# Pairs of experts in one result bank: zero columns in the stationary operand, split weights in the common buffers, a smaller gather, and a shift that VectorE adds

## The chip, the core and the metric

One core of one Trainium2 chip runs the whole program. The metric is the device time of one execution in microseconds (us). The engines are TensorE (PE, with its weight loads as PEld), VectorE (DVE), ScalarE (ACT), GpSimd (POOL) and SyncE (SP), which issues the transfers (DMA) of the weights.

## What is computed

Two transformer blocks on 256 tokens of 1024 features. The first mixes three branches and has a dense feed-forward layer; the second has two kinds of attention and a mixture of 32 experts, and the change lies in that last part. Each token goes to the best of 4 groups and there to its best 2 of 8 experts:

```python
h2 = _modulate(_rmsnorm(x, g_ffn), shift_ffn, scale_ffn)       # x * gain + shift, per feature
group = argmax(h2 @ w_group);  top_p, top_local = top_k(softmax(expert logits of the group), 2)
y[dest] = (silu(xb @ w_gate[e]) * (xb @ w_up[e])) @ w_down[e]   # 1024 -> 512 -> 1024, every expert e
x = x + gate_ffn * (weighted sum of each token's two expert rows)
```

All is float32. The weights of the experts are 32 x 6 pieces of 1 MiB.

## The kernel before

**Weights as a stream of units.** `PLAN` lists 319 units, each 128 x 2048 float32 (1 MiB), in the order of their use; the last 192 are those of the experts. I number these 0 to 191. They come as: 8 units of gate and up weights of a pair of experts (2 + 2 for each of the two), then 4 units of down weights of the pair before, and so on; so a pair has 12 units. `prefetch` (L295) issues one transfer per unit on SP while fewer than `st["cap"]` raw units are held and the pool `units` (18 buffers, `NS`) has one free. The cap is 13 before the experts and 7 in them (L1249, L1549).

**Two parts of a weight.** PE multiplies rounded operands (fp32r) in one pass. So that nothing is lost, `convert_unit` (L330) splits a unit: ACT writes `hi`, the rounded weight, and DVE writes `lo = raw - hi` (L345). Then each unit is used by 4 matmuls with `hi` and 4 with `lo`, 128 x 512 of weights moving in each. `hi` has 3 buffers, `lo` 2, in a pool of their own, `pairs`. The function `whole` (L290) names the units that are not split: PE multiplies them as plain float32, by 8 matmul instructions that take longer. It picks units 13, 37, 61, ..., eight in all.

**An expert's rows.** An expert has 32 slots for tokens. `gather` (L1408) multiplies the normed tokens (`hth`, `htl`, rounded part and remainder) by a matrix of zeros and ones (`oh`, made by DVE) and so brings the rows of 8 experts at once into `xg`: 32 columns of rounded parts and 32 of remainders per expert, 64 columns in all. These 64 columns stand still in PE while the weights move, so a result has 64 partitions. `gate_up` (L1476) writes the gate and up results of one expert into one bank each (`pe`), and ACT copies each to `gy` (64 x 512). `hidden` (L1489) folds the two halves of a pair together on PE (`pT`), and ACT and DVE make `hs`, the input of the down weights. `down` (L1510) writes two banks per expert (`pd`), and ACT copies them to `gy`.

**Other work between the units.** Generators in the list `bg` are pulled one step at each half unit: `gather` of the next 8 experts (every 4 pairs), `put_weights` (the routing weights, every 4 pairs), and `put_back` (L1526), which after every 4 pairs returns 4 pairs' results to the tokens by 64 float32 matmul instructions (`py`); DVE adds these to `x` (L1539). Copies and sums that wait for PE are put off by `post` for a number of half units.

**Order.** The order on each engine is made by a scheduler when the program is built, within the dependences and the buffers; SP keeps the order in which the code issues. Each engine works strictly in that order.

**Before the experts.** The routing stretch computes the logits, picks groups and experts on DVE, and makes the normed tokens: for each of four tiles, 4 matmuls of `x` with a diagonal of gains (`dg`) and one matmul that adds the shift (`std` times `shift_row`, one row), then `hth` on ACT and `htl` on DVE straight from the bank (L1359 to L1370).

Of the kernel before, what the change touches and what calls it, by code (L numbers as in the profile page):

```python
# [213 lines left out]
def block_kernel(ctx: ExitStack, tc: tile.TileContext, A, out):  # L214
# [75 lines left out]
    def whole(u):  # L290

        m = u - MOE0
        return m < NU - MOE0 - 4 and m % 24 == 13
# [36 lines left out]
    def convert_unit(parts=1):  # L330
# [20 lines left out]
    def take_unit(*name):  # L351
# [14 lines left out]
        if whole(u):  # L366
            raw.pop(u)
            free()

# [850 lines left out]
    shift_row = gains[0:1, 1024:]  # L1220
    gains = gains[:, :1024].rearrange("p (k f) -> p k f", k=8)
    for k in range(8):
        V.tensor_scalar(gains[:, k], ident, gm[:, 1, k:k + 1], None, op0=OP.mult)
    for k4 in range(2):
        p = ps("pb")
        for i in range(4):
            k = 4 * k4 + i
            mm(p[:1, i * 128:(i + 1) * 128], mod[:, 24 + k:25 + k], ident, start=True, stop=True)
        V.tensor_copy(shift_row[:, k4 * 512:(k4 + 1) * 512], p[:1])
# [19 lines left out]
    st["cap"] = 13  # L1249
# [121 lines left out]
    free()  # L1371
# [35 lines left out]

    def gather(g):  # L1408

        oh = [t256("oh", F32R) for tt in range(2)]  # L1410
        for tt in range(2):
            t1 = t256("oh1")
            V.tensor_scalar(t1, slot, slg[g][:, 0, tt:tt + 1], None, op0=OP.is_equal)
            last["oh"] = V.scalar_tensor_tensor(oh[tt], slot, slg[g][:, 1, tt:tt + 1], t1,
                                                op0=OP.is_equal, op1=OP.add).ins
        yield
        xs = [unit("xg", F32R).rearrange("p (e k c) -> p e k c", e=4, k=8) for i in range(2)]
        xg[2 * g], xg[2 * g + 1] = xs
        yield
        for k in range(8):  # L1420
            p = ps("pg")
            for i, h in enumerate((hth, htl)):
                for tt in range(2):
                    mm(p[:, i * 256:(i + 1) * 256], h[:, tt, k * 128:(k + 1) * 128], oh[tt],
                       start=i + tt == 0, stop=tt == 1, skip_group_check=True)

            def keep(k=k, p=p):
                pv = p.rearrange("p (i e r) -> p i e r", i=2, e=8)
                for i in range(2):
                    last["xg"] = act(xs[i][:, :, k].rearrange("p e (i r) -> p i e r", i=2), pv[:, :, 4 * i:4 * i + 4],  # L1430
                                     AF.Copy)
# [43 lines left out]

    def gate_up(e):  # L1476
        xs = xg[e // 4][:, e % 4]
        for i, nm in enumerate(("eg", "eu")):
            p = ps("pe")
# [3 lines left out]
            if e % 4 == 0 and not i:  # L1483
                g = unit("gy")
                gy[e // 2], gy[e // 2 + 1] = g[:, :1024], g[:, 1024:]
            t = gy[e // 2][(e % 2) * 64:(e % 2) * 64 + 64]
            post(lambda i=i, p=p, t=t: act(t[:, i * 512:(i + 1) * 512], p[:64], AF.Copy))

    def hidden(q):  # L1489
# [13 lines left out]
        def parts():  # L1503
            act(hs[:, :, :, 0], sv, AF.Copy)
            V.tensor_sub(hs[:, :, :, 1], sv, hs[:, :, :, 0])  # L1505
        post(product, 2)
        post(parts, 4)
        return hs.rearrange("p f e i r -> p f e (i r)")

    def down(e, hs):  # L1510
        pd = [ps("pd"), ps("pd")]
        for k2 in range(2):
            for ws in take_unit("ed", e, k2):
                rows_times([(pd[n][:64], hs[:, 2 * k2 + i, e % 2], 2 * i + n, k2 + i == 0, k2 + i == 2)
                            for i in range(2) for n in range(2)])(ws)
        y = gy[e // 2][(e % 2) * 64:(e % 2) * 64 + 64]

        def keep():
            for n in range(2):
                if n and e == NE - 1:  # L1520
                    V.tensor_copy(y[:, n * 512:(n + 1) * 512], pd[n][:64])
                else:
                    act(y[:, n * 512:(n + 1) * 512], pd[n][:64], AF.Copy)
        post(keep)
# [33 lines left out]
    for p in range(NE // 2 + 1):  # L1558
# [153 lines left out]
```

## Time and profile before

| | us |
|---|---|
| median of 3 runs | 1336.34 (1331.66 to 1337.39) |
| the profiled execution's own time | 1338.32 |
| its span in the trace | 1336.5 |
| PE / DVE / ACT / POOL busy in the span | 1215.3 / 1045.3 / 840.4 / 101.6 |
| bytes read | 338.88 MB |

Busy time of PE runs from a matmul's start to its modelled end, and neighbours overlap; the spacing of starts tells more. The experts' stretch, from the first matmul with an expert's weights to the last of `put_back`, lies between 755 and 1317 us. No engine is busy all of that time, so the waits have to be read beside the busy time.

### The profile page before, as it was taken

The page shows a single profiled execution, that of the slowest core. Times are in us where ns is not written, and L with a number is a line of the kernel's source. Part 1 is how long each engine was busy: PE and PEld are TensorE (multiplying, and loading weights), DVE is VectorE, ACT ScalarE, POOL GpSimd, SP SyncE. Part 2 cuts the span into 40 slices and gives each one's busy share as a digit, 9 for nine tenths or more (in the row PEclk, how much of TensorE's full clock was granted, in tenths as well). Part 3 has the DMA queues.
Part 4 walks back from the last instruction along what each step waited for, and adds up shares of the span by engine and source line. Part 5 has one row for each costly group of instructions (what it writes and reads, how often), then busy time and mean ns, then how long its engine had stood idle before and what let it go on. Part 6 is the DMA issues. An engine that isn't in the chain of part 4 may idle for free. (4 is left out here: it accounts for less than half of the span.)

```text
span 1336.5 us, 19007 instructions
## 1 busy us (share of the span) xinstructions
PE 1215.3 (91%) x7468; PEld 966.8 (72%) x7468; DVE 1045.3 (78%) x1215; ACT 840.4 (63%) x983; POOL 101.6 (8%) x102
## 2 busy tenths in 40 slices
PE   6996999999999999889999989989898988889885
PEld 6984899989999999788888645546554655456454
DVE  6799999967898887766456597986797669867874
ACT  5576545384644444554554589985887679767872
POOL 2569200200000000000000000000000000000000
PEclk8899999999999999898998799999899999999998
DMA  9632356547698885231171297998799879989921
GB/s 364 257 126 94 138 224 212 190 164 287 257 339 335 318 320 229 86 136 64 50 280 81 107 382 299 400 421 347 272 391 398 316 285 376 423 328 354 421 108 33
DMA packets 48621, 341.21 MB, mean 255 GB/s; under 512 B 5392, under 2 KB 5648, under 8 KB 7824
## 3 DMA queue, kind: packets, MB, share of 16 engines
q1 hardware_dynamic: 47664, 337.65, 65.3%
q10 hardware_dynamic: 864, 2.31, 0.5%
q8 instruction: 60, 0.98, 0.3%
q14 instruction: 33, 0.27, 0.1%
HBM read 338.88 MB, written 1.05 MB: 254 GB/s over the span
## 5 line engine op out<-in xcount | busy, mean ns | idle before, releaser
L221 ACT ACTIVATE hi<-raw 128x1024 fp32r<-128x1024 f32 (+1 forms) x392 | 562.4, 1456 | 300.2 <-issue 46.7
L345 DVE TENSOR_TENSOR lo<-raw,hi 128x2048 fp32r<-128x2048 f32 (+1 forms) x186 | 414.9, 2264 | 100.7 <-ACT hi L221 39.5
L323 DVE TENSOR_TENSOR lo<-raw,hi 128x1024 fp32r<-128x1024 f32 x206 | 260.2, 1270 | 77.6 <-ACT hi L221 77.2
L237 PE MATMUL pe<-lo,xg 128*64 128x512 f32 x480 | 133.3, 402 | 19.8 <-DVE lo L345 18.6
L237 PE MATMUL pe<-hi,xg 128*64 128x512 f32 x480 | 131.0, 401 | 7.7 <-ACT hi L221 7.7
L237 PEld LDWEIGHTS pe<-lo,xg 128*64 128x64 f32 x480 | 60.3, 135 | 76.7 <-DVE lo L345 39.2
L237 PEld LDWEIGHTS pe<-hi,xg 128*64 128x64 f32 x480 | 63.6, 136 | 57.1 <-ACT hi L221 14.2
L630 DVE SCALAR_TENSOR_TENSOR ca<-ch,par,ca 128x246 f32<-128x246 f32 (+25 forms) x180 | 101.2, 590 | 0.9
L237 PE MATMUL pd<-lo,hs 128*64 128x512 f32 x256 | 73.9, 414 | 13.5 <-DVE lo L345 12.6
L1689 POOL TENSOR_TENSOR x<-x,rstd 128x512 f32<-128x512 f32 x1 | 1.7, 1717 | 1057.3 <-DVE rstd L496 1057.3
L237 PE MATMUL pd<-hi,hs 128*64 128x512 f32 x256 | 73.3, 413 | 8.4 <-DVE hs L1505 4.5
L237 PEld LDWEIGHTS pd<-lo,hs 128*64 128x64 f32 x256 | 33.4, 139 | 47.5 <-DVE lo L345 28.5
L237 PE MATMUL py<-ws,gy 128*128 128x256 f32 x256 | 60.4, 392 | 4.5 <-PEq L1598 4.1
L237 PEld LDWEIGHTS pd<-hi,hs 128*64 128x64 f32 x256 | 34.8, 140 | 36.1 <-ACT hi L221 8.6
L237 PEld LDWEIGHTS py<-ws,gy 128*128 128x128 f32 x256 | 50.5, 198 | 14.0 <-issue 4.9
L621 POOL TENSOR_TENSOR ca<-ca,tap 128x255 f32<-128x255 f32 (+29 forms) x60 | 56.5, 944 | 35.9 <-ACT tap L221 32.3
L314 DVE SCALAR_TENSOR_TENSOR raw<-raw,aux 128x1024 f32<-128x1024 f32 x48 | 56.8, 1219 | 0.0
L221 ACT ACTIVATE gy<-pe 64x512 f32<-64x512 f32 x64 | 37.9, 592 | 27.0 <-PE pe L237 26.0
L237 PE MATMUL pgt<-nh,hi 128*128 128x256 f32 x192 | 54.3, 283 | 0.0
L237 PE MATMUL pgt<-nl,hi 128*128 128x256 f32 x192 | 54.1, 282 | 0.0
L237 PE MATMUL pgt<-nh,lo 128*128 128x256 f32 x192 | 53.8, 280 | 0.0
L221 ACT ACTIVATE gy<-pd 64x512 f32<-64x512 f32 x63 | 34.3, 583 | 29.3 <-PE pd L237 29.1
(345 smaller groups left out, 3019.2 us busy)
## 6 DMA issues: line engine op xcount, KB each, us to landing
raw<-in_ws_dram SPq DMA_DIRECT2D x318, 1024.0 KB, 7.0
x<-in_xt_dram SPq DMA_DIRECT2D x4, 256.0 KB, 4.3
raw<-in_ws_dram SPq DMA_DIRECT2D x2, 512.0 KB, 8.9
out_dram<-x SPq DMA_DIRECT2D x4, 256.0 KB, 2.7
aux<-in_sguw_dram ACTq DMA_DIRECT2D x1, 512.0 KB, 9.7
aux<-in_cnt_dram SPq DMA_DIRECT2D x1, 512.0 KB, 12.6
aux<-in_sgub_dram ACTq DMA_DIRECT2D x1, 512.0 KB, 3.9
aux<-in_cvec_dram ACTq DMA_DIRECT2D x1, 512.0 KB, 4.7
```

The costliest lines, as they stand in the source:

```text
L221: ins = S.activation(out, in_, func, **k).ins
L237: last["mm"] = T.matmul(*a, **k).ins
L314: V.scalar_tensor_tensor(r, r, 1.0, cond["c"], op0=OP.mult, op1=OP.mult, accum_out=mod[:, col:col + 1])
L323: st["lo"] = V.tensor_sub(lo, r, hi).ins
L345: st["lo"] = V.tensor_sub(lo[:, c], raw[u][:, c], hi[:, c]).ins
L621: G.tensor_tensor(ca[:, j, d:], ca[:, j, d:], t[:, :256 - d], op=OP.add)
L630: V.scalar_tensor_tensor(ca[:, j, d:], ch[:, j, :256 - d], w(30 - d), ca[:, j, d:], op0=OP.mult, op1=OP.add)
L1689: (G if k2 == 3 else V).tensor_tensor(x2, x2, over2(r), op=OP.mult)
```

## The change

Six edits go together.

1. **Pairs in one bank.** The rows of a pair stand in 192 columns (`xs`): 64 of the even expert, 64 zeros, 64 of the odd one. `window` takes 128 of them: rows and zeros for the even expert, zeros and rows for the odd one. Both experts' matmuls then accumulate into the same 128 partitions of a bank, and ACT copies a bank once per pair, 128 x 512. The input of the down weights (`hsz`) is laid out in the same way. GpSimd writes the zeros once.
2. **Split parts in the common buffers.** `hi` and `lo` are taken from `units`; each split unit holds two buffers until its matmuls are issued. The buffers of `xg` are no longer taken from there. The caps are 10 and 5 for 13 and 7.
3. **Whole units.** Units 9, 25, 41, ..., twelve in all, are not split.
4. **Gather per four experts**, every 2 pairs; the `oh` of eight experts is still made at once. A gather matmul moves 128 columns for 256, and there are 256 of them for 128.
5. **Shift.** The one-row matmul goes. The shift stands in all partitions (made by PE and ACT in the attention stretch), DVE adds it to the scaled tile (`row`), and ACT and DVE split `row` (`keep_rows`).
6. Some copies and `put_back` are put off by one or two half units more.

```diff
     def whole(u):
-        return m < NU - MOE0 - 4 and m % 24 == 13
+        return m < NU - MOE0 - 4 and m % 16 == 9
...
-            hi = pairs.tile([P, 2048], F32R, name="hi", tag="hi", bufs=3)
-            lo = pairs.tile([P, 2048], F32R, name="lo", tag="lo", bufs=2)
+            hi, lo = unit("hi", F32R), unit("lo", F32R)
...
+            t = t256("sd", shape=(P, P))
+            V.tensor_scalar(t, ident, mod[:, 24 + k:25 + k], None, op0=OP.mult)
+            mm(p[:, i * 128:(i + 1) * 128], one1, t, start=True, stop=True)
+        act(shift[:, k4 * 512:(k4 + 1) * 512], p, AF.Copy)
...
-    st["cap"] = 13
+    st["cap"] = 10
...
-                mm(p, std[:, tt * 128:(tt + 1) * 128], shift_row[:, k4 * 512:(k4 + 1) * 512], start=False, stop=True,
-                   skip_group_check=True)
-            act(hth[:, tt, c], p, AF.Copy, scale=rk[:, tt:tt + 1])
-            V.scalar_tensor_tensor(htl[:, tt, c], p, rk[:, tt:tt + 1], hth[:, tt, c], op0=OP.mult, op1=OP.subtract)
+    def keep_rows():
+        for k4, tt, p in rows:
+            t = t512("row")
+            V.scalar_tensor_tensor(t, p, rk[:, tt:tt + 1], shift[:, c], op0=OP.mult, op1=OP.add)
+            split_act(t, hth[:, tt, c], htl[:, tt, c])
...
+    xs = [pairs.tile([P, 8, 2, 192], F32R, name="xs", tag=f"xs{i}", bufs=1) for i in range(2)]
+    hsz = [pairs.tile([P, 4, 192], F32R, name="hsz", tag=f"hsz{i}", bufs=1) for i in range(2)]
...
+        oh = [t[:, (g % 2) * 128:(g % 2 + 1) * 128] for t in ohs[g // 2]]
+        for k2 in range(4):
+            for kk in range(2):
+                k = 2 * k2 + kk
+                for i, h in enumerate((hth, htl)):
+                    c = slice(kk * 256 + i * 128, kk * 256 + (i + 1) * 128)
+                    for tt in range(2):
+                        mm(p[:, c], h[:, tt, k * 128:(k + 1) * 128], oh[tt],
+                           start=kk + i + tt == 0, stop=tt == 1, skip_group_check=True)
...
+    def window(t, e):
+        return t[:, (e % 2) * 64:(e % 2) * 64 + 128]
...
-                    rows_times([(p[:64], xs[:, 4 * k2 + k], k, k2 + k == 0, k2 + k == 4) for k in range(4)])(ws)
-            post(lambda i=i, p=p, t=t: act(t[:, i * 512:(i + 1) * 512], p[:64], AF.Copy))
+                    rows_times([(p, window(x4[:, 4 * k2 + k], e), k, not odd and k2 + k == 0, odd and k2 + k == 4)
+                                for k in range(4)])(ws)
+        if odd:
+            for i in range(2):
+                post(lambda i=i, p=pes[q][i]: act(gy[q][:, i * 512:(i + 1) * 512], p, AF.Copy), i + 2)
...
-    st["cap"] = 7
+    st["cap"] = 5
...
+            if p % 2 == 0 and p < NE // 2 - 2:
+                bg.append(gather(p // 2 + 1))
```

Three places in the order of the built programs follow. Numbers at the names are buffers.

**PE in the routing stretch.** `pT` is the bank of a tile of the normed tokens, `dg` the diagonal of gains, `prk` the ranks of the picked experts. Before:

```order
L237 MATMUL pT_7686<-dg_6949,x_75 128x128 x4
L237 MATMUL pT_7686<-dg_6949,std_7634 128x512
L237 MATMUL pT_7694<-dg_6949,x_75 128x128 x4
L237 MATMUL pT_7694<-dg_6949,std_7634 128x512
L237 MATMUL prk_7660<-rt_7648,cst_91 128x32
L237 MATMUL prk_7660<-rt_7648,one1_103 128x32
L237 MATMUL prk_7660<-rt_7648,cst_91 128x32 x2
```

Now:

```order
L237 MATMUL pT_7696<-dg_6949,x_75 128x128 x4
L237 MATMUL pT_7701<-dg_6949,x_75 128x128 x4
L237 MATMUL prk_7670<-rt_7658,cst_91 128x32
L237 MATMUL prk_7670<-rt_7658,one1_103 128x32
L237 MATMUL prk_7670<-rt_7658,cst_91 128x32 x2
```

The one-row matmuls with `std` are gone, two ahead of the ranks and two behind them.

**ACT at units 90 to 95** (of the down weights and then of the next pair's gate weights). `hi` from `raw` is a rounded weight, `gy` from `pd` or `pe` a copied result. Before:

```order
L221 ACTIVATE hi_9480<-raw_9359 128x2048
L221 ACTIVATE gy_9155<-pd_9478 64x512
L221 ACTIVATE gy_9155<-pd_9479 64x512
L221 ACTIVATE hi_9495<-raw_9384 128x2048
L221 ACTIVATE hi_9511<-raw_9421 128x2048
L221 ACTIVATE gy_9155<-pd_9509 64x512
L221 ACTIVATE gy_9155<-pd_9510 64x512
L221 ACTIVATE hi_9527<-raw_9438 128x2048
L221 ACTIVATE hi_9542<-raw_9447 128x2048
L221 ACTIVATE hi_9558<-raw_9453 128x2048
```

Now:

```order
L221 ACTIVATE hi_9472<-raw_9384 128x2048
L221 ACTIVATE hi_9487<-raw_9408 128x2048
L221 ACTIVATE hi_9500<-raw_9434 128x2048
L221 ACTIVATE gy_9207<-pd_9470 128x512
L221 ACTIVATE gy_9207<-pd_9471 128x512
L221 ACTIVATE hi_9514<-raw_9452 128x2048
L221 ACTIVATE hi_9530<-raw_9476 128x2048
L221 ACTIVATE hi_9546<-raw_9491 128x2048
```

Four copies have become two, and they stand behind the `hi` of the third unit.

**DVE at a gather.** `oh` is the matrix that a gather moves. Before (units 66 to 69):

```order
L345 TENSOR_TENSOR lo_8998<-raw_8853,hi_8997 128x2048
L1413 TENSOR_SCALAR oh1_9006<-cst_91,rt_7648 128x256
L345 TENSOR_TENSOR lo_9023<-raw_8890,hi_9022 128x2048
L1414 SCALAR_TENSOR_TENSOR oh_9004<-cst_91,rt_7648,oh1_9006 128x256
L1413 TENSOR_SCALAR oh1_9009<-cst_91,rt_7648 128x256
L1414 SCALAR_TENSOR_TENSOR oh_9005<-cst_91,rt_7648,oh1_9009 128x256
L345 TENSOR_TENSOR lo_9049<-raw_8938,hi_9048 128x2048
```

Now (units 78 to 80):

```order
L344 TENSOR_TENSOR lo_9211<-raw_9153,hi_9210 128x2048
L1431 TENSOR_SCALAR oh1_9218<-cst_91,rt_7658 128x256
L1431 TENSOR_SCALAR oh1_9221<-cst_91,rt_7658 128x256
L1432 SCALAR_TENSOR_TENSOR oh_9216<-cst_91,rt_7658,oh1_9218 128x256
L1432 SCALAR_TENSOR_TENSOR oh_9217<-cst_91,rt_7658,oh1_9221 128x256
L344 TENSOR_TENSOR lo_9234<-raw_9169,hi_9233 128x2048
```

A split no longer stands between the four operations, and the gather has moved from the pair behind a `put_back` to the next pair.

## Rows read from the trace of the kernel before

**Rows 1.** Stretches of the experts' part and, last, of the routing: busy time of each engine (and instructions), granted PE clock, DMA share, GB/s; in us from the start of the span.

```profile
755.00:1313.00 558.00, 495.92 (x2170) 293.78 (x2169) 446.54 (x291) 433.37 (x404) 0.00 (x0) 0.98 0.85 335
...
771.00:898.00 127.00, 111.92 (x503) 64.36 (x501) 113.69 (x76) 110.91 (x106) 0.00 (x0) 0.99 0.94 375
898.00:950.00 52.00, 48.07 (x208) 32.82 (x207) 33.82 (x27) 31.16 (x29) 0.00 (x0) 0.90 0.84 326
950.00:1045.00 95.00, 81.82 (x349) 43.92 (x348) 79.94 (x48) 79.12 (x78) 0.00 (x0) 0.98 0.94 368
1045.00:1094.00 49.00, 45.08 (x206) 30.84 (x205) 33.28 (x27) 31.03 (x29) 0.00 (x0) 0.97 0.85 311
1094.00:1189.00 95.00, 80.56 (x348) 43.44 (x347) 80.37 (x48) 79.66 (x78) 0.00 (x0) 0.99 0.94 371
1189.00:1229.00 40.00, 39.66 (x172) 26.58 (x171) 26.68 (x21) 25.43 (x21) 0.00 (x0) 0.97 0.86 320
1229.00:1298.00 69.00, 59.10 (x259) 32.70 (x258) 56.20 (x32) 55.62 (x48) 0.00 (x0) 1.00 0.73 301
...
1284.00:1313.00 29.00, 26.89 (x126) 18.67 (x126) 19.86 (x19) 16.50 (x15) 0.00 (x0) 1.00 0.00 1
...
850.00:900.00 50.00, 43.98 (x179) 23.27 (x178) 44.44 (x23) 42.90 (x37) 0.00 (x0) 0.98 1.01 417
...
731.00:750.00 19.00, 19.00 (x56) 12.07 (x55) 9.99 (x56) 2.36 (x5) 0.00 (x0) 0.50 0.00 0
```

**Rows 2.** Groups of instructions by line and form in the whole span: busy us, mean ns of one, idle time before them.

```profile
L345 DVE TENSOR_TENSOR lo<-raw,hi 128x2048 fp32r<-128x2048 f32 x182 | 410.1, 2287 | 100.7 <-ACT hi L221 39.5 <-PE pe L237 38.0 <-PE pd L237 10.7
L221 ACT ACTIVATE hi<-raw 128x2048 fp32r<-128x2048 f32 x182 | 342.5, 1916 | 63.1 <-PE pe L237 44.9 <-PE pd L237 16.5 <-DVE lo L345 0.8
...
L237 PEld LDWEIGHTS pe<-hi,xg 128*64 128x64 f32 x480 | 63.6, 136 | 57.1 <-ACT hi L221 14.2 <-issue 2.4
...
L237 PEld LDWEIGHTS py<-ws,gy 128*128 128x128 f32 x256 | 50.5, 198 | 14.0 <-issue 4.9 <-ACT gy L221 0.9
...
L221 ACT ACTIVATE gy<-pe 64x512 f32<-64x512 f32 x64 | 37.9, 592 | 27.0 <-PE pe L237 26.0 <-DVE lo L345 0.6
...
L221 ACT ACTIVATE gy<-pd 64x512 f32<-64x512 f32 x63 | 34.3, 583 | 29.3 <-PE pd L237 29.1
```

**Rows 3.** Who waited for whom between 755 and 1313 us: us in total, times, longest.

```profile
DVE lo L345 <- ACT hi L221: 39.5, 27, 2.3
...
ACT gy L221 <- PE pe L237: 26.0, 26, 2.5
ACT gy L221 <- PE pd L237: 23.6, 15, 4.7
...
PEld pg L237 <- DVE oh L1414: 13.2, 3, 4.4
...
DVE lo L345 <- DMA raw<-in_ws_dram: 3.3, 2, 2.3
```

**Rows 4.** Instructions in order of time at units 91 to 93, with the idle time before each and what ended it in brackets.

```profile
1008.57 1.07 ACT L221 ACTIVATE gy<-pd 64x512 f32<-64x512 f32 x2 [1.52 <-PE pd L237]
...
1009.66 5.52 ACT L221 ACTIVATE hi<-raw 128x2048 fp32r<-128x2048 f32 x3
...
1011.61 4.49 DVE L345 TENSOR_TENSOR lo<-raw,hi 128x2048 fp32r<-128x2048 f32 x2 [1.84 <-ACT hi L221]
```

**Rows 5.** The same view at the first `put_back` and the gather behind it.

```profile
900.16 5.38 PE L237 MATMUL py<-ws,gy 128*128 128x256 f32 x22
...
910.87 1.91 ACT L221 ACTIVATE hi<-raw 128x2048 fp32r<-128x2048 f32 x1 [5.99 <-PE pe L237]
...
939.86 1.01 PE L237 MATMUL pg<-oh,hth 128*128 128x256 f32 x3 [3.93 <-DVE oh L1414]
```

**Rows 6.** PE in the routing stretch, in order of time; a float32 matmul is two instructions.

```profile
731.32 2.08 PE L237 MATMUL pT<-dg,x 128*128 128x128 f32 x8
733.33 2.07 PE L237 MATMUL pT<-dg,std 1*128 1x512 f32 x2
...
747.91 2.07 PE L237 MATMUL pT<-dg,std 1*128 1x512 f32 x2
749.91 1.44 PE L237 MATMUL pg<-oh,hth 128*128 128x256 f32 x5
```

**Rows 7.** PE elsewhere, in order of time: units with 64 and with 128 standing columns, a whole unit (`raw`), transposes of 128 columns, and the gather.

```profile
652.07 0.40 PE L237 MATMUL pv<-hi,hl 128*128 128x512 f32 x1
652.31 0.39 PE L237 MATMUL pv<-lo,hh 128*128 128x512 f32 x1
...
654.63 0.49 PE L1159 MATMUL pT<-cst,et 128*128 128x128 f32 x3
...
754.57 0.28 PE L237 MATMUL pg<-oh,htl 128*128 128x256 f32 x1
754.69 0.28 PE L237 MATMUL pg<-oh,hth 128*128 128x256 f32 x1
...
849.55 1.08 PE L237 MATMUL pe<-lo,xg 128*64 128x512 f32 x4
850.47 1.08 PE L237 MATMUL pe<-hi,xg 128*64 128x512 f32 x4
...
852.41 3.65 PE L237 MATMUL pe<-raw,xg 128*64 128x512 f32 x8
```

More of the change, by code (lines that the diff above doesn't have):

```diff
@@ L1219, in block_kernel @@
     gains = unit("dg")
-    shift_row = gains[0:1, 1024:]
+    shift = gains[:, 1024:]
     gains = gains[:, :1024].rearrange("p (k f) -> p k f", k=8)
@@ L1357, in block_kernel @@
     ranked = last["mm"]
+    rows = []
     for k4 in range(2):
@@ L1406, in block_kernel @@
     xg, wsel = {}, {}
-    def gather(g):
[L1410 to L1420, printed above, removed]
-            p = ps("pg")
[L1422 to L1431, printed above, removed]
+    xs = [pairs.tile([P, 8, 2, 192], F32R, name="xs", tag=f"xs{i}", bufs=1) for i in range(2)]
@@ new lines, in block_kernel, with keep @@
+    hsz = [pairs.tile([P, 4, 192], F32R, name="hsz", tag=f"hsz{i}", bufs=1) for i in range(2)]
+    for t in xs:
+        G.memset(t[:, :, :, 64:128].bitcast(F32), 0.0)
+    for t in hsz:
+        G.memset(t[:, :, 64:128].bitcast(F32), 0.0)
+    ohs = {}
+    def gather(g):
+        if g % 2 == 0:
+            oh = ohs[g // 2] = [pairs.tile([P, 256], F32R, name="oh", tag="oh", bufs=4) for tt in range(2)]
+            for tt in range(2):
+                t1 = t256("oh1")
+                V.tensor_scalar(t1, slot, slg[g // 2][:, 0, tt:tt + 1], None, op0=OP.is_equal)
+                last["oh"] = V.scalar_tensor_tensor(oh[tt], slot, slg[g // 2][:, 1, tt:tt + 1], t1,
+                                                    op0=OP.is_equal, op1=OP.add).ins
+            yield
+            yield
+        oh = [t[:, (g % 2) * 128:(g % 2 + 1) * 128] for t in ohs[g // 2]]
+        for k2 in range(4):
+            p = ps("pg")
+            for kk in range(2):
+                k = 2 * k2 + kk
+                for i, h in enumerate((hth, htl)):
+                    c = slice(kk * 256 + i * 128, kk * 256 + (i + 1) * 128)
+                    for tt in range(2):
+                        mm(p[:, c], h[:, tt, k * 128:(k + 1) * 128], oh[tt],
+                           start=kk + i + tt == 0, stop=tt == 1, skip_group_check=True)
+            def keep(k2=k2, p=p):
+                pv = p.rearrange("p (k i a b r) -> p k i a b r", k=2, i=2, a=2, b=2)
+                for kk in range(2):
+                    o = xs[g % 2][:, 2 * k2 + kk].rearrange("p a (h i r) -> p a h i r", h=3, i=2)
+                    last["xg"] = act(o[:, :, 0:3:2], pv[:, kk].rearrange("p i a b r -> p a b i r"), AF.Copy)
@@ L1503, in parts, with keep @@
         def parts():
-            act(hs[:, :, :, 0], sv, AF.Copy)
-            V.tensor_sub(hs[:, :, :, 1], sv, hs[:, :, :, 0])
+            act(ho[:, :, 0:3:2, 0], sv, AF.Copy)
+            V.tensor_sub(ho[:, :, 0:3:2, 1], sv, ho[:, :, 0:3:2, 0])
         post(product, 2)
         post(parts, 4)
-        return hs.rearrange("p f e i r -> p f e (i r)")
+        return hs
+    pds = []
     def down(e, hs):
-        pd = [ps("pd"), ps("pd")]
+        odd = e % 2 == 1
+        if not odd:
+            pds[:] = [ps("pd"), ps("pd")]
         for k2 in range(2):
             for ws in take_unit("ed", e, k2):
[L1514 to L1524, printed above, removed]
+                rows_times([(pds[n], window(hs[:, 2 * k2 + i], e), 2 * i + n, not odd and k2 + i == 0,
+                             odd and k2 + i == 2) for i in range(2) for n in range(2)])(ws)
+        if odd:
+            y = gy[e // 2]
+            def keep(pd=list(pds)):
+                for n in range(2):
+                    if n and e == NE - 1:
+                        V.tensor_copy(y[:, n * 512:(n + 1) * 512], pd[n])
+                    else:
+                        act(y[:, n * 512:(n + 1) * 512], pd[n], AF.Copy)
+            post(keep, 2)
     def put_back(qs, after=None):
@@ L1568, in block_kernel @@
             gate_up(2 * p + 1)
-            if p % 2 == 1:
-                free()
-            if p % 4 == 1 and p // 4 < 3:
-                bg.append(gather(p // 4 + 1))
+            if p % 2 == 0 and p < NE // 2 - 2:
+                bg.append(gather(p // 2 + 1))
             if p % 4 == 2 and p // 4 < 3:
                 bg.append(put_weights(p // 4 + 1))
-            if p % 4 == 3:
+            if p % 2 == 1:
                 drain()
```

30 lines of the change are left out of this document (18 added, 12 removed).

## The prediction

> **What bounds the kernel now.** I read the table of stretches first, since the change lies in the experts' part and that part alternates. From 755 to 1313 us PE is busy 496 of 558 us, DVE 447, ACT 433, and the DMA engines 0.85 of the time [rows 1]. None of them bounds it alone; four engines at 78 to 89% with two or three buffers between them wait for each other in turn.
>
> The stretches show three kinds. In B (771 to 898) and D (950 to 1045, 1094 to 1189, 1229 to 1298) DVE is busy 80 to 90% and PE 85 to 88%. In C, the three stretches with a `put_back` (898 to 950, 1045 to 1094, 1189 to 1229), PE is busy 92 to 99% and DVE only 65 to 68% [rows 1]. So PE bounds C, and DVE and ACT with their hand-overs bound B and D.
>
> The groups of instructions give the price of a unit: 1.92 us of ACT for `hi`, 2.29 us of DVE for `lo`, and 0.59 us of ACT for each copy of a result, 127 of them [rows 2]. The table of waits tells where DVE loses time in B and D: it waits 39.5 us for ACT's `hi`, and ACT itself waits 26.0 and 23.6 us in front of copies whose matmuls have not ended [rows 3]. The order of time shows that loop at unit 92: ACT waits 1.52 us for PE before two copies, then starts `hi`, and DVE has stood 1.84 us when it gets it [rows 4]. The weights hardly count: DVE waited 3.3 us for a transfer [rows 3].
>
> In C the engine behind PE is stopped: `put_back` holds PE in pieces of 5.4 us, and ACT waits 6.0 us for a buffer [rows 5]. Behind the first two of them comes a gather whose `oh` stands on DVE behind a split that waits for PE; PE stands 3.9 us for it there, and the row of waits has 13.2 us for three such places [rows 3, 5].
>
> **The parts, worked out.** The profiled execution took 1338.3 us, 2.0 over the median; I sum against it and take 2 off at the end.
>
> *Routing.* PE runs without a break to the first gather at 749.9, and each one-row matmul of the shift takes 2.0 us of that [rows 6]. Four go: 8.0 us. In their place DVE adds the shift and splits the tile. I estimate 0.57 us for 512 columns from `lo` (2.29 us for 2048) [rows 2]. Two additions, two splits and, by the new order, the `lo` of unit 2 now stand ahead of the second pick, which PE needs: 4 x 0.57 + 2.29 = 4.6 us. So between 3.4 and 8.0 us are gained; I take **-5**. The zeros are written by POOL, which has nothing to do in the experts' part [rows 1], and are needed only after the routing: 0. The shift in the attention stretch has as many float32 matmuls as before, eight small DVE operations and two copies by ACT for two by DVE: 0, within 3 either way.
>
> *Copies.* 127 of 64 x 512 become 64 of 128 x 512. A longer one should cost between a quarter of `hi` (0.48 us) and the same 0.59 us [rows 2]; I take 0.59, the nearer row. That frees some 37 us of ACT, off the path by itself. What counts is that half of the places at which ACT waits for PE vanish, and that the others stand a unit later in the new order.
>
> *Whole units.* Four more: DVE -4 x 2.29 = -9 us, ACT -8, PE +4 x (3.65 - 1.84) = +7, where 1.84 is two groups of four matmuls, 0.92 us apart [rows 2, 7].
>
> *Gather.* Matmuls of 128 moving fp32r columns are not in this trace. Below, 128-column transposes follow each other every 0.11 us (three in 0.49, the last 0.27 of it); above, plain float32 of 128 columns takes 2.0 us for four in the routing, where the granted clock is 0.50, the level of 1.2 GHz, so 0.25 each at 2.4 GHz [rows 1, 6, 7]. The nearest is the gather itself with 256 columns, 0.12 [rows 7], so I take 0.11. Then a gather of four experts costs 32 x 0.11 = 3.5 us, as much as one of eight did. Seven instead of three in the stretch: PE +14 us.
>
> *B, 127 us.* PE: 111.9 + 1.8 (a whole unit more) + 5.9 (2¾ gathers for one) = 120; DVE: 113.7 - 2.3 = 111; transfers: 48 units of 1.05 MB at the best rate, 417 GB/s, 2.51 us each = 121 [rows 1]. I take 122: **-5**.
>
> *D, 259 us.* DVE stands 42 us in the three stretches [rows 1]. PE goes from 81.8 to 87 in the two of 95 us (a gather and a quarter, and most of a whole unit); transfers need 36 x 2.51 = 90 less the five units that a C stretch leaves in stock. I take 89.5, 89.5 and 65: **-15**, about a third of DVE's waits.
>
> *C, 141 us.* The third has no gather and takes 40 us [rows 1]; the first two lose theirs to other places, where it is counted above, and come to 41 and 40, the third to 39: **-21**.
>
> Sum: 1338.3 - 5 - 5 - 15 - 21 = 1292.3, less 2.0: **1290**.
>
> *Buffers.* Three transfers less are made ahead of the experts, 7.5 us of DMA time that moves into the stretch, and a raw unit is held 7 or 8 units ahead for 9. Both are hidden by the stock that keeps DVE from waiting for DMA [rows 3]; without that cover it is the second rival. SP's queue waits for PE as well as DVE now, since freed `hi` and `lo` become raw buffers; only transfers stand behind such a wait. By the buffers' places in the built program a `lo` mostly takes the place of the `hi` two units before, so DVE still can't run far ahead of a `put_back`; that is why I leave C at 39 to 41.
>
> *Weight loads, a rule against the change.* Loading 64 columns takes 136 ns, 128 columns 198 [rows 2]. Matmuls of 512 columns follow each other every 0.23 us with 64 standing columns and every 0.24 with 128 [rows 7]: the load is hidden, and I count nothing. The Trainium skill (TensorE: Matmul & The Clock Gate, LDWEIGHTS) says that a load takes time by its columns, so 53 ns more here; unhidden, by that page, an estimate of 76 us over 1440 matmuls, and the sum would be 1366. The rows decide for the hidden load.
>
> **Rivals.** *Gather at the float32 rate* (0.25 us): 256 x 0.14 = 36 us more on PE. B's PE comes to 132, so B takes 132, +10; PE in the long D comes to 93 and they to 94, +4.5 each; the gather before the first unit +5: 1290 + 24 = **1314**. For it: nothing here has fewer than 256 columns in fp32r. Against: 512 and 256 columns run at the same rate per column [rows 7]. Chance 0.17.
>
> *The transfers become the bound.* If 182 units come at B's mean rate of 375 GB/s from 752 us on, they end at 752 + 182 x 1.049 / 0.375 = 1261; no bytes move after 1284 now, and the span ends 52.5 us after that [rows 1], so 1314 for the span and **1314** for the median (1.8 us lie around a span, 2.0 come off). For it: shares of 0.94 in B and D. Against: 417 GB/s was reached, and the stock was never empty. 0.12.
>
> *Nothing moves but the ends.* If DVE's waits come from PE's use of `lo` and not from the copies, B and D stay, C gives its 8 us of waiting for `oh`, and the additional gathers cost that back: 1338 - 5 = **1331** by the median. 0.08.
>
> *Slower.* If the load of 128 columns shows: 1440 x 62 ns = 89 us more on PE, beside 7 and 14 of the other edits; 496 + 110 = 606 for 558 us, less the 5 of routing: 1338 + 43 - 2 = **1379**. It decides as soon as the spacing grows by (62 - 21) / 1440 = 0.03 us, since PE has 62 us of slack. For it: loads are 46% longer. Against: the spacing in rows 7. 0.06.
>
> **How the numbers follow.** 0.57 is left for the forecast. Its own bounds: routing -8, B 119, D 235, C 118 give 1338.3 - 8 - 8 - 24 - 23 - 2 = 1273; its slow side meets the two rivals at 1314. The range is 1270 to 1322, with some room on both sides of these, and the last two rivals out. A difference under 0.5% (7 us) can't be told from none. Faster by more: 0.57 + 0.17 + 0.12 = 0.86; same 0.08; slower 0.06.
>
> **What would show it.** The profile after: `gy` copies of 128x512 x64 near 0.6 us and ACT's waits before them under 25 us; DVE waiting for `hi` under 25; the first matmul of unit 0 at about 750; no PE wait for `oh` over 1 us; 12 whole units; 128-column gathers 0.11 us apart; spacing of the experts' matmuls still 0.23. I am wrong if DVE waits for transfers by more than 15 us, if the spacing grows, or if the stretches D stay at 95.

## The result, and the profile after

The changed kernel takes **1296.8 us** (median; 1292.3 to 1301.0) where the kernel before takes 1336.7 on the same chip: a ratio of 0.971, 95% interval 0.967 to 0.975. Run again on another chip it took 1293.7 us, ratio 0.9715 (0.969 to 0.974). The forecast was 1290, range 1270 to 1322.

The profiled execution of the changed kernel took 1301.0 us (span 1299.2), 37.3 less than the one of before; the points below are summed between these two. The stretches of the experts' part, cut at the same units as in [rows 1]; columns as there, with PE, PEld, DVE, ACT, POOL, then clock, DMA share, GB/s:

```profile
762.00:888.00 126.00, 120.74 (x567) 92.69 (x566) 108.24 (x71) 100.86 (x97) 0.00 (x0) 0.99 0.99 403
888.00:926.50 38.50, 38.50 (x173) 31.12 (x172) 28.58 (x22) 24.33 (x18) 0.00 (x0) 1.00 0.76 283
926.50:1020.60 94.10, 88.81 (x414) 67.06 (x413) 82.55 (x53) 75.10 (x71) 0.00 (x0) 1.00 1.01 416
1020.60:1059.20 38.60, 38.60 (x173) 31.23 (x172) 28.69 (x22) 24.43 (x18) 0.00 (x0) 1.00 0.78 295
1059.20:1153.40 94.20, 88.91 (x414) 67.12 (x414) 82.47 (x53) 75.12 (x71) 0.00 (x0) 1.00 1.01 413
1153.40:1192.00 38.60, 38.60 (x173) 31.22 (x172) 28.69 (x22) 24.41 (x18) 0.00 (x0) 1.00 0.80 289
1192.00:1257.00 65.00, 59.64 (x250) 43.50 (x250) 53.11 (x29) 45.48 (x37) 0.00 (x0) 0.97 0.94 392
...
746.00:1274.00 528.00, 506.60 (x2305) 391.05 (x2305) 437.24 (x291) 390.44 (x342) 0.00 (x0) 0.99 0.90 362
```

The stretches with a `put_back` are all 38.6 us now, PE without a gap. The long ones have hardly moved (126 and twice 94 for 127 and twice 95), but what fills them has: PE stands 5.3 us in each, where it stood 13 to 15, and the DMA engines are at a share of 0.99 to 1.01.

The groups that answer to [rows 2], busy us, mean ns of one, and idle time before them; then the copies from the view of the tile `gy` (ns, shortest, median and longest):

```profile
L344 DVE TENSOR_TENSOR lo<-raw,hi 128x2048 fp32r<-128x2048 f32 x178 | 401.7, 2288 | 73.6 <-ACT hi L221 72.6
...
L221 ACT ACTIVATE hi<-raw 128x2048 fp32r<-128x2048 f32 x178 | 335.3, 1920 | 64.0 <-PE pe L237 22.9 <-DVE lo L344 21.4 <-PE py L237 7.4
...
L237 PEld LDWEIGHTS pe<-hi,xs 128*128 128x128 f32 x480 | 89.8, 191 | 31.1 <-ACT hi L221 9.5 <-issue 1.7 <-ACT xs L221 0.3
```

```profile
L221 ACT ACTIVATE gy<-pe x32: 572/598/694, 760.4 to 1245.4; 128x512 f32<-128x512 f32 x32
L221 ACT ACTIVATE gy<-pd x31: 580/597/658, 794.3 to 1273.9; 128x512 f32<-128x512 f32 x31
```

A copy of 128 rows takes 0.60 us, as one of 64 did. DVE's waits for PE ahead of a `lo`, 48.7 us in [rows 2], are gone; those for `hi` are 72.6 where they were 39.5. The table of waits between 747 and 1280 us (us in total, times, longest) says where ACT is late:

```profile
DVE lo L344 <- ACT hi L221: 72.6, 64, 3.8
PEld pe L237 <- DVE lo L344: 26.1, 36, 1.6
ACT gy L221 <- PE pd L237: 24.8, 9, 10.5
...
ACT sgm L221 <- PE pT L237: 22.7, 11, 4.2
...
ACT xs L221 <- PE pg L237: 11.5, 9, 2.1
...
ACT gy L221 <- PE pe L237: 10.6, 6, 2.2
...
ACT hi L221 <- DMA raw<-in_ws_dram: 6.5, 12, 1.2
```

Two rows of the kernel before that were not shown, from the same view and the same stretch of time:

```profile
ACT sgm L221 <- PE pT L237: 3.8, 6, 1.2
...
ACT xg L221 <- PE pg L237: 2.0, 2, 1.1
```

So ACT's waits in front of `gy` fell from 26.0 and 23.6 [rows 3] to 10.6 and 24.8, of which 10.5 is one wait at the very end; but those in front of `sgm` (the hidden rows, from `pT`) and of the gather's copies (`xs` now, `xg` before) grew from 5.8 to 34.2. There are half as many copies of `gy`, and ACT waits for PE in front of copies as long as ever: 69.6 us, or 59.1 without the wait at the end, for 55.4.

One such place, at unit 92, in order of time on ACT, DVE and PE (idle time before a row and what ended it in brackets):

```profile
983.16 1.92 ACT L221 ACTIVATE hi<-raw 128x2048 fp32r<-128x2048 f32 x1 [1.45 <-PE pd L237]
986.67 1.09 ACT L221 ACTIVATE gy<-pd 128x512 f32<-128x512 f32 x2 [1.59 <-PE pd L237]
987.64 5.52 ACT L221 ACTIVATE hi<-raw 128x2048 fp32r<-128x2048 f32 x3
```

```profile
989.59 6.69 DVE L344 TENSOR_TENSOR lo<-raw,hi 128x2048 fp32r<-128x2048 f32 x3 [2.19 <-ACT hi L221]
```

```profile
989.61 1.19 PE L237 MATMUL pe<-hi,xs 128*128 128x512 f32 x4 [0.88 <-ACT hi L221]
991.93 1.20 PE L237 MATMUL pe<-lo,xs 128*128 128x512 f32 x4 [1.13 <-DVE lo L344]
```

ACT has made `hi` 92, which itself waited 1.45 us for PE, and then stands before two copies until PE has finished unit 91 at 986.7. `hi` 93 stands behind them and begins at 987.64. PE has unit 92 alone for these three microseconds, and then waits 0.88 for `hi` and 1.13 for `lo` of 93: 2.0 of its 5.3 us in this stretch. A gap of 1.12 or 1.13 us stands at the same place of the plan, 48 units apart, in B and in the next D too.

Right behind a `put_back` it is another thing that ACT waits for:

```profile
938.31 1.91 ACT L221 ACTIVATE hi<-raw 128x2048 fp32r<-128x2048 f32 x1 [0.60 <-DMA raw<-in_ws_dram]
940.79 1.91 ACT L221 ACTIVATE hi<-raw 128x2048 fp32r<-128x2048 f32 x1 [0.57 <-DMA raw<-in_ws_dram]
```

Here `hi` follows the landing of its weights, one in 2.5 us.

The routing and the first matmuls, by PE in order of time: the ranks, the gather ahead of unit 0 and its rest behind it, and units with 128 standing columns:

```profile
734.34 0.64 PE L237 MATMUL prk<-rt,cst 128*128 128x32 f32 x2 [1.78 <-DVE rt L1347]
...
738.40 0.64 PE L237 MATMUL prk<-rt,cst 128*128 128x32 f32 x2 [2.56 <-DVE rt L1347]
...
743.12 0.88 PE L237 MATMUL pg<-oh,hth 128*128 128x128 f32 x3
...
746.10 0.27 PE L237 MATMUL pg<-oh,htl 128*128 128x128 f32 x1
746.21 0.28 PE L237 MATMUL pg<-oh,hth 128*128 128x128 f32 x1
...
746.43 1.85 PE L237 MATMUL pe<-hi,xs 128*128 128x512 f32 x7
...
750.23 0.22 PE L237 MATMUL pg<-oh,htl 128*128 128x128 f32 x1
...
756.43 1.10 PE L237 MATMUL pe<-lo,xs 128*128 128x512 f32 x4
757.37 1.10 PE L237 MATMUL pe<-hi,xs 128*128 128x512 f32 x4
758.31 1.09 PE L237 MATMUL pe<-lo,xs 128*128 128x512 f32 x4
```

The gather begins at 743.1, 6.8 us earlier than in [rows 6], and a matmul of 128 moving columns takes 0.11 us (granted clock 1.00 from 745.0 to 746.4, the level of 2.4 GHz). Only 22 of its 32 matmuls stand ahead of unit 0; the other ten follow from 750.23. PE no longer runs without a break through the routing: it waits 1.78 and 2.56 us for DVE's `rt`, the picks, ahead of the ranks. A group of four experts' matmuls takes 0.94 us, 0.235 each, where it was 0.92 and 0.23 [rows 7].

### The profile page after: what moved, and what is told of

Same layout as the page of the kernel before. It is cut to its first block, busy times and chain, and to the rows that moved or that the text cites. A ratio compares the mean times of both kernels' runs of the same rounds, so it can differ in the third digit from the quotient of the medians.

```text
span 1299.2 us, 19089 instructions
## 1 busy us (share of the span) xinstructions
PE 1216.7 (94%) x7588; PEld 1062.1 (82%) x7588; DVE 1039.4 (80%) x1221; ACT 797.7 (61%) x917; POOL 104.4 (8%) x106
## 5 line engine op out<-in xcount | busy, mean ns | idle before, releaser
L344 DVE TENSOR_TENSOR lo<-raw,hi 128x2048 fp32r<-128x2048 f32 (+1 forms) x182 | 406.4, 2264 | 73.6 <-ACT hi L221 72.6
L237 PE MATMUL pe<-lo,xs 128*128 128x512 f32 x480 | 138.3, 411 | 11.7 <-DVE lo L344 10.7
L237 PE MATMUL pe<-hi,xs 128*128 128x512 f32 x480 | 137.4, 409 | 4.6 <-ACT hi L221 4.0
L237 PEld LDWEIGHTS pe<-lo,xs 128*128 128x128 f32 x480 | 87.1, 190 | 43.8 <-DVE lo L344 26.1
L237 PEld LDWEIGHTS pe<-hi,xs 128*128 128x128 f32 x480 | 89.8, 191 | 31.1 <-ACT hi L221 9.5
L237 PE MATMUL pd<-lo,hsz 128*128 128x512 f32 x240 | 67.4, 402 | 5.1 <-DVE lo L344 4.9
L237 PE MATMUL pd<-hi,hsz 128*128 128x512 f32 x240 | 68.1, 405 | 0.0
L237 PEld LDWEIGHTS py<-ws,gy 128*128 128x128 f32 x256 | 50.1, 196 | 14.2 <-issue 6.7
L237 PEld LDWEIGHTS pd<-hi,hsz 128*128 128x128 f32 x240 | 45.0, 188 | 12.9 <-issue 1.9
L237 PE MATMUL pfg<-xh,hi 128*128 128x256 f32 x176 | 49.7, 282 | 0.0
L237 PE MATMUL pfg<-xl,hi 128*128 128x256 f32 x176 | 49.5, 281 | 0.0
L237 PE MATMUL pfg<-xh,lo 128*128 128x256 f32 x176 | 49.5, 281 | 0.0
```

The lines of the kernel that those rows point to most:

```text
L237: last["mm"] = T.matmul(*a, **k).ins
L344: st["lo"] = V.tensor_sub(lo[:, c], raw[u][:, c], hi[:, c]).ins
```

## The experiments

Times are medians; each ratio is against the kernel before on the same chip, with its 95% interval. The changed kernel's own is 0.9715 (0.969 to 0.974). What a run takes more or less is the difference of the ratios, in us of the kernel before; each is uncertain by 3 to 5 us (run 8's by 7).

**1. The shift by PE again.**

```diff
-            t = t256("sd", shape=(P, P))
-            V.tensor_scalar(t, ident, mod[:, 24 + k:25 + k], None, op0=OP.mult)
-            mm(p[:, i * 128:(i + 1) * 128], one1, t, start=True, stop=True)
+            mm(p[:1, i * 128:(i + 1) * 128], mod[:, 24 + k:25 + k], ident, start=True, stop=True)
...
+                mm(p, std[:, tt * 128:(tt + 1) * 128], shift_row[:, k4 * 512:(k4 + 1) * 512], start=False, stop=True,
+                   skip_group_check=True)
...
-    keep_rows()
```

> The changed kernel with the shift added by PE again, as before (a matmul from one row, copies fused with it); the rest of the change stays. Theory A: unit 0 began 9.4 us earlier in the changed kernel, 6.8 of it ahead of the first gather (749.9 to 743.1) and 2.6 in the gather itself, which is for four experts now; so this kernel takes 6.8 us more, 1304 us, its unit 0 begins near 753 and its first gather near 750. Rival: the whole 9.4 comes from the shift: 1306, unit 0 near 756. Second rival: the later start is made up again by a fuller stock of raw units: 1297.

1304.4 us, ratio 0.978 (0.975 to 0.980): 8 more. Four matmuls of one row, 2.07 us each, are 8.3. This lies between theory A's 6.8 and its first rival's 9.4 and does not part them; that the later start is made up again is out. The profile does not part them either. Its first gather begins at 746.2 and unit 0 at 751.0, both earlier than theory A put them, but unit 8 is 7.6 us later than in the changed kernel (769.7 for 762.1): PE's granted clock is 0.50 in it from unit 0 to 758.4, where the changed kernel has 1.00 from unit 0 on.

**2. Eight whole units.**

```diff
-        return m < NU - MOE0 - 4 and m % 16 == 9
+        return m < NU - MOE0 - 4 and m % 24 == 13
```

> The changed kernel with 8 whole units in place of 12 (every 24th, as before). Theory A: PE bounds the experts' stretch now (506.6 us busy of 528); four units less at 3.6 us instead of 1.87 take 7 us off PE: 1290 us. Rival B: DVE and ACT with their hand-overs bound it: four more splits (2.26 us of DVE, 1.9 of ACT) cost up to 9 us: 1302 to 1306. Rival C: transfers bound it: 1297, no change.

1301.3 us, ratio 0.976 (0.974 to 0.979): some 6 slower. The long stretch of 94.1 us takes 96.2 with PE busy 89.4 of it: one whole unit less, which is less work for PE, doesn't help, and one split more on DVE and ACT costs its 2 us. Theory A, that PE alone bounds, is out.

**3. One transfer in eight left out.**

```diff
+    def again(u):
+        return u >= MOE0 and (u - MOE0) % 8 == 7
...
+            if again(u):
+                raw[u] = raw[u - 1]
```

> The changed kernel without one in eight of the experts' transfers: that unit takes its weights from the raw buffer of the unit ahead of it, and is split and multiplied as ever. Theory A: PE bounds the stretch and its 21 us of waits are at places where a split stands behind another hand-over, not behind a transfer: 1297 us, within 4. Rival C: the stretches behind a put_back are bound by the transfers (ACT began hi 0.1 us after landing at units 74 to 80, 123 to 128 and 166 to 179): 37 units for 94 us become 33, D goes to PE's own 89 us, 1277 to 1287 us.

1273.8 us, ratio 0.957 (0.954 to 0.960): 20 less by the ratios (23 by the medians), and D at 87.5. It looks like theory C. But the scheduler (the planner, in the expectations) sets each engine's order by when it thinks things are ready, and with other transfers it had set ACT another order: `gy` stands behind `hi` 93 here, where it stood behind 92. On ACT, in order of time:

```profile
966.26 3.76 ACT L221 ACTIVATE hi<-raw 128x2048 fp32r<-128x2048 f32 x2
971.53 1.92 ACT L221 ACTIVATE hi<-raw 128x2048 fp32r<-128x2048 f32 x1 [1.51 <-PE pd L237]
974.11 1.09 ACT L221 ACTIVATE gy<-pd 128x512 f32<-128x512 f32 x2 [0.66 <-PE pd L237]
```

So this run changed two things at once; runs 9 to 11 set the order by hand.

**4. The copies' time given back.** Each copy is made in two of 64 rows, at the same place in the code.

```diff
+    def halves_of(o, p):
+        for h in range(2):
+            act(o[64 * h:64 * h + 64], p[64 * h:64 * h + 64], AF.Copy)
```

> The changed kernel with each copy of a result made as two copies of 64 x 512, one behind the other: the work of ACT is again what it was before the change (some 38 us more), but the places where ACT waits for PE stay halved. Theory A: it is the number of places at which ACT waits for PE that counted, not the time of the copies, since PE bounds: 1300 us, up to 1305. Rival: the time of the copies is what was gained: PE's waits, which fell from 53 to 21 us in the stretches between the put_backs, come back: 1320 to 1330.

1317.0 us, ratio 0.988 (0.986 to 0.991): 22 more, nearer to the rival than to theory A. The stretch that answers to D:

```profile
930.30:1028.30 98.00, 89.43 (x409) 67.17 (x408) 82.06 (x53) 84.80 (x82) 0.00 (x0) 0.98 0.98 394
```

ACT is busy 85 of 98 us, for 75 of 94. So the time of the copies counts, though ACT is not the busiest engine. But the 22 us need not be the time's alone: the scheduler set ACT another order here too. Of the 31 copies from `pd`, eight stand one `hi` later than in the changed kernel and five one earlier, and those from `pT` one later in seven places of 16. What an order can be worth is measured in runs 9 and 10, 8 to 11 us; how much of the 22 it is here is not shown.

**5. The changed kernel again**, as a control.

> The changed kernel again, beside the three others of this call: 1297 us by every theory (1292 to 1301), and unit 0 at 746 or some 5 us earlier, as in two of the runs before it.

1293.7 us. Its profiled execution has unit 0 at 742.6, 4 us earlier than the other, with the same stretches of 38.5 and 94.1 us. The last stretch takes 62.3 us at a granted clock of 1.00, where the other took 65.0 at 0.97. So the two profiles of one program differ by 4 us ahead of unit 0 and by 3 in the last stretch, and C and D not at all.

**6. Each put_back spread.**

```diff
+                if not i:
+                    for _ in range(4):
+                        yield
...
-            yield
+            for _ in range(4):
+                yield
...
-            if p % 2 == 1:
+            if p % 4 == 3:
                 drain()
```

> The changed kernel with each put_back of the stretch in eight pieces of 2.7 us, one for two units of weights, in place of four of 5.4 us at one place. No work is added or left out. Theory C (transfers set the pace of B and D, and stand idle for a quarter of the 38.6 us of each put_back stretch, since the raw buffers there are full): a good half of these 27 us is won back, 1280 to 1287 us, and the DMA share over the experts' stretch goes from 0.90 to 0.94 or more. Theory A (PE is the bound, its work is the same): 1293 to 1297. Rival on the other side: copies and adds of the pieces now stand in front of splits on ACT and DVE, which have less slack there than inside the put_back stretch: 1300 to 1308.

1294.3 us, ratio 0.973 (0.970 to 0.976): no change. The two stretches, `put_back` and D:

```profile
918.20:1014.60 96.40, 91.12 (x425) 69.28 (x424) 82.72 (x55) 76.24 (x71) 0.00 (x0) 1.00 0.99 395
882.00:918.20 36.20, 36.20 (x162) 29.01 (x161) 28.05 (x20) 23.56 (x18) 0.00 (x0) 1.00 0.92 337
```

The DMA engines are busy 0.92 in the `put_back` stretch now, for 0.76; the pair takes 132.6 us for 132.6 (38.5 + 94.1). Idle transfers there did not set the pace. (Six of the 31 copies from `pd` stand two `hi` earlier here; run 12, with the copies' places held, is the cleaner test.)

**7. The kernel before, with its gathers a pair (12 units) later** and nothing else: the expectation says four, but they begin at units 29, 77 and 125 for 17, 65 and 113.

```diff
-            if p % 4 == 1 and p // 4 < 3:
+            if p % 4 == 2 and p // 4 < 3:
                 bg.append(gather(p // 4 + 1))
```

> The kernel before, with nothing but its gathers (of eight experts, as they were) begun four units after the place where they stood behind a put_back. Theory G: the first two put_back stretches lose the gather and the wait for its one-hot tiles and shrink from 51 and 49 us to the 40 of the third; the stretches behind them take the gather's 4 us each, and the one ahead of them takes it too: 1336 - 19 + 8 to 12, 1325 to 1329 us. Rival: the stretches behind give all of it back, since transfers that ran during the wait are missing there: 1336. Second rival: the long put_back stretches came from the form of the gather, not from its place, and stay: 1336 as well, with stretches of 50 us.

1324.5 us, ratio 0.993 (0.991 to 0.996): 9 less.

```profile
894.60:934.90 40.30, 39.93 (x177) 26.74 (x178) 28.74 (x21) 25.89 (x22) 0.00 (x0) 1.00 0.93 374
934.90:1034.40 99.50, 84.25 (x382) 47.47 (x381) 85.54 (x55) 84.37 (x84) 0.00 (x0) 1.00 0.94 377
```

The `put_back` stretch goes from 51 to 40 us, and the one behind it from 95 to 99.5: theory G. The place of the gather is what shortens the stretch, and the stretches behind give part of it back, so that 9 us are left of about 20. PE's waits for `oh` go with the gather and stay: 9.2 us in three places, for 13.2 [rows 3].

**8. Splits one unit ahead, seven raw buffers.**

```diff
-        while st["mconv"] <= min(u + 2, NU - 1):
+        while st["mconv"] <= min(u + 1, NU - 1):
...
-    st["cap"] = 5
+    st["cap"] = 7
```

> The changed kernel with splits one unit ahead of the matmuls in place of two, and seven raw buffers in place of five: the same memory as more transfers and fewer splits ahead. Theory C (transfers set the pace): two more raw units lie ready when a put_back ends, and the transfers run on for 5 us more in each: 1285 to 1292 us. Rival (the splits' hand-overs set it, and the shared buffers gained by letting DVE run ahead of PE): the waits of DVE for PE that the change removed come back, 48.7 us of them before, and a good part of them lands on PE: 1310 to 1335 us.

1311.8 us, ratio 0.986 (0.981 to 0.991): some 19 more. The rival's time: what is split ahead is worth more than what is loaded ahead. But not by the waits that it named: DVE's for PE ahead of a `lo` are 2.9 us, and it is ACT's `hi` that waits for units with PE, 50.1 us for 22.9.

**9 to 11. ACT's copies later in its order.** The instructions are the same; `gy`, `sgm`, `hsz` and `xs` are kept behind a `hi` that was issued before them. In run 9 this moves 12 of the 32 copies from `pe`, 8 of the 31 from `pd` and 11 of the 16 `sgm`, most by one or two `hi`; the others stood late enough.

```diff
+    def behind(*a, **k):
+        with tc.issue_after(st["his"][-2]):
+            return act(*a, **k)
...
-                post(lambda i=i, p=pes[q][i]: act(gy[q][:, i * 512:(i + 1) * 512], p, AF.Copy), i + 2)
+                post(lambda i=i, p=pes[q][i]: behind(gy[q][:, i * 512:(i + 1) * 512], p, AF.Copy), i + 2)
```

Run 10 has [-1] for [-2]; run 11 is run 9 with the transfers of run 3.

> The changed kernel with its instructions as they are, and ACT's copies of results (gy, sgm, hsz, xs) kept in order behind the hi that was issued last but one when they fall due: most stand one hi later than the planner put them (gy of the stretch behind hi 93 in place of 92, sgm behind 72 and 97 in place of 71 and 95). The left-out transfers of an earlier run had changed this order as well, so its 23 us may have come from either. Theory O (ACT stands at a copy until PE has finished the unit that it multiplies, and the next hi stands behind it, so that PE has nothing ready when it gets there): the 5 us of PE's waits in each of B and D go, 1278 to 1285 us, D at 90, and ACT's waits for PE before copies fall by half. Theory C (transfers set the pace): no change, 1294 to 1297.

> The same with the copies behind the last hi that was issued, two hi later than the planner put most of them. Theory O: as much as one hi later or somewhat more on ACT's side, but the hidden rows come later to the down matmuls, which PE then waits for at two places for eight units: 1277 to 1287 us. Theory C: 1294 to 1297.

> One hi later and, besides, one in eight of the experts' transfers left out (its unit takes the weights of the unit ahead of it), with nearly the same order on ACT as in the run one hi later. Theory O: the transfers add little to the order: within 5 us of the run one hi later, near 1275. Theory C: the 23 us of the left-out transfers come on top of whatever the order gives: 1272 here, and 1294 without them.

Run 9: **1286.3 us**, ratio 0.965 (0.964 to 0.967). Run 10: **1283.3**, 0.963 (0.962 to 0.965). Run 11: 1266.0, 0.950 (0.949 to 0.952). The place of unit 92 and 93 in run 9, on ACT and on PE:

```profile
974.92 3.79 ACT L221 ACTIVATE hi<-raw 128x2048 fp32r<-128x2048 f32 x2 [2.87 <-PE pd L237]
978.62 1.06 ACT L221 ACTIVATE gy<-pd 128x512 f32<-128x512 f32 x2
```

```profile
978.47 1.10 PE L237 MATMUL pe<-hi,xs 128*128 128x512 f32 x4
979.40 1.09 PE L237 MATMUL pe<-lo,xs 128*128 128x512 f32 x4
980.33 1.09 PE L237 MATMUL pe<-hi,xs 128*128 128x512 f32 x4
981.42 1.20 PE L237 MATMUL pe<-lo,xs 128*128 128x512 f32 x4
```

ACT makes `hi` 92 and 93 and comes to the copies when PE is done with them; it doesn't wait there, and PE loses no more than 0.2 us at unit 93. In all, ACT's waits for PE in front of copies fall from 69.6 us to 30.4, of which 16.1 is the one at the end; those of `hi` for a unit that PE still reads (`pe`) grow from 22.9 to 40.4. The stretch D of runs 9 and 10 and of run 11, and the transfers in run 9's table of waits:

```profile
918.20:1008.70 90.50, 87.61 (x414) 67.54 (x413) 81.63 (x53) 75.04 (x71) 0.00 (x0) 1.00 1.01 422
```

```profile
915.90:1005.20 89.30, 87.25 (x414) 67.52 (x412) 80.96 (x53) 74.88 (x67) 0.00 (x0) 1.00 1.01 422
```

```profile
912.00:998.90 86.90, 85.84 (x414) 67.87 (x412) 80.97 (x53) 74.70 (x71) 0.00 (x0) 1.00 0.97 382
```

```profile
ACT hi L221 <- DMA raw<-in_ws_dram: 18.7, 24, 2.6
```

Both theories hold a part. The order alone is worth 8 to 11 us, as theory O had it. It takes 4 or 5 off each of the two long D and as much off B; the last stretch gains nothing (65.3 and 65.2). With the order mended, ACT waits for transfers (18.7 us for 6.5), the DMA engines are full at 422 GB/s, and leaving out one transfer in eight takes 20 us more; there theory O's "within 5" was wrong. Here too the order moved along: 12 more of the copies of run 11 stand late than of run 9, and against run 10 it is 17. The two gains add: 8 and 20 us apart, 28 together.

**12. Both edits that leave the work whole**: run 10 with the spread `put_back` of run 6.

> Copies two hi later, as in the run that took 1283.3 us, and each put_back in eight pieces of 2.7 us, one for two units; all work is done. Theory OC (order and transfers each hold part of the time: the order is mended, so the transfers bind in D, and the DMA engines' idle share in the put_back stretches is worth something now): 1272 to 1278 us, DMA share over the experts' stretch up from 0.90 to 0.93 or more. Rival (spreading gives nothing now as it gave nothing alone, since PE needs its 501 us of 518 in any case): 1281 to 1285.

1280.0 us, ratio 0.961 (0.958 to 0.964), the fastest that computes everything; its interval overlaps run 10's. D and the `put_back` stretch are 91.7 and 36.4, 128.1 together as in run 10 (89.3 + 38.7), though ACT's waits for transfers went from 14.7 to 4.1 us. A gain from spreading is not shown.

## Why the prediction was right, and which steps were not

The time is 7 us above the forecast. That it came so near is in part luck: the largest term fell 14 us short, and two others gave 8 more than forecast. Term by term, between the two profiled executions, with the stretches of before cut at the same units as those of now (B 126.9; C 51.1, 48.8, 40.4; D 95.1, 95.1, 68.5):

*Routing: -5 forecast, -9.3 measured* (unit 0 at 746.43 for 755.77). The trace parts it in three. From PE's first `pT` to the gather it is 14.3 us for 18.6, 4.3 less: the four one-row matmuls gave their 8, and PE waits 4.3 us for DVE's picks, where it waited for nothing. That is near the subtraction that I made (4.6), and the term as I meant it was right in size. (In run 1, without DVE's additions, 2.6 us of such waits stay: the `lo` of unit 2 stands ahead of the second pick there too.) The other 5 us I had not looked at. The first `pT` begins 2.5 us earlier; before, PE waited 1.95 us ahead of it for squares that stood on DVE behind two `lo`. And unit 0 follows 3.3 us behind the gather's start for 5.9, since ten of the 32 matmuls come behind its first ones and the granted clock rises from 0.50 to 1.00 after 1.6 us of the gather, not after 4.4. The start of unit 0 differs by 4 us in run 5, so the size of these two is not firm. Run 1 gives the shift 8 us, without parting the terms.

*C: -21 forecast, -25 measured* (38.5, 38.6, 38.6). Right, and for the reason given; run 7 makes the same stretch short with that edit alone. It is not a net gain: in run 7 the stretches behind took back more than half.

*B and D: -20 forecast, -6 measured* (B 127 to 126; D 95, 95, 69 to 94, 94, 65; with the clock of run 5 the last would be 62). Here the step failed. PE's work came as reckoned: 120.7 us where I had 120, 88.8 where I had 87. I then let the waits shrink to 2 or 2.5 us a stretch, and they are 5.3. Three sentences of the prediction are at fault.

- "That frees some 37 us of ACT, off the path by itself." Run 4 gave this time back to ACT and took 22 us more, a part of which may be its other order. So the time of the copies was on the path in part.
- "What counts is that half of the places at which ACT waits for PE vanish, and that the others stand a unit later in the new order." The copies did become half. But I looked at the `gy` copies only. `sgm` and the gather's copies stand in the same in-order queue, and they took over the waits, 34 us for 6. With one `hi` ahead of such a copy, PE runs dry behind it. Runs 9 and 10 get 8 to 11 us back by order alone.
- "transfers need 36 x 2.51 = 90 less the five units that a C stretch leaves in stock." A short C adds nothing to the stock. It moves 283 GB/s x 38.5 us / 1.049 MB = 10.4 units and uses 12; in the kernel before it moved 326 x 52 / 1.049 = 16 [rows 1]. So D has to bring 36 + 1.6 = 37.6 units, which at 416 GB/s is 95 us, about what it takes, and ACT stands for landings at its head. But this is a coincidence of two limits, not the bound alone: with the `put_back` spread, so that 337 GB/s x 36.2 us / 1.049 MB = 11.6 units came in its stretch, the pair of stretches took as long (run 6), and with the order mended alone D took 90.5 (run 9).

*The end of the program* took 3 us more (42.2 us behind the last stretch, for 39.0), which I had not looked at.

Sum of what was measured, with the start of unit 8 (762.0 for 771.6) in place of that of unit 0: -9.6 - 24.6 - 6.3 + 3.2 = -37.3.

*The rivals.* The gather at the float32 rate is out: 0.11 us. The unhidden load is out: the spacing grew by 0.005 us, some 7 us over 1440 matmuls, where a load has 55 ns more. The Trainium skill (TensorE: Matmul & The Clock Gate, LDWEIGHTS) has a load's time go by its columns. The trace agrees that it grows, from 136 to 191 ns; this stays hidden but for some 7 of 79 us. That nothing moves but the ends came near for B and D, for another reason than I gave: their waits were exchanged, not kept. And the transfers: as the only bound they would have given 1314, which didn't come; as one of two limits they hold a part of the time, as runs 9 and 11 show.

Of the marks that I named, the copies, the twelve whole units, the gather's spacing and the missing wait for `oh` came. Unit 0 came earlier. ACT's waits before `gy` (35, "under 25") and DVE's for `hi` (73, "under 25") did not, and D at 94 is nearly the sign that I had set for being wrong.

What is left open: why leaving out transfers is worth 20 us when their waits can be taken away (run 12) without a gain. Run 11 differs from run 10 most in the last stretch (58.9 us for 65.2), and a shared raw buffer also holds two units' stock; neither was tried by itself. Of the six edits, the shift, the whole units, the copies and the gather's place were tried, at 8, 6, 22 and 9 us. They sum to 45, each uncertain by 3 to 5, for 40 in all. The common buffers for `hi` and `lo`, with which DVE's waits for PE went, the smaller gather and the later posts were not undone by themselves; what they are worth is not shown.

## What to carry to other kernels

When an engine works in order, a copy that waits for PE costs what stands behind it: count all the kinds of copies in that queue, not only the one that is edited, and ask how many units PE has ready when the copy comes up. When a stall is taken out of one stretch, ask what ran under it: here transfers did, and the next stretch had to bring them (bringing them earlier again gained nothing in runs 6 and 12, so ask the second question too: what else holds that stretch). A total near the forecast does not confirm its terms: sum them one by one. And an experiment that changes what a scheduler sees changes its order, as in runs 3, 4, 6 and 11: compare the order before reading the time.

## What had not been expected of the hardware

The DMA engines held 422 GB/s for a whole stretch of 90 us (run 9), above the 417 that the trace of before had shown in its best stretch [rows 1]. The matmuls with 128 standing columns follow each other 0.005 us later than those with 64. And between two executions of one program the part ahead of the experts differs by 4 us and the last stretch by 3 (granted clock 0.97 for 1.00), while D repeats to 0.1 us.
